# Unscaled expert queries, norm chains in PSUM, compact score copies in four pieces and position additions on GpSimd, in a two-block transformer kernel

## The chip, the cores and the metric

The kernel runs on one core of a Trainium2 chip, as one program. The metric is its device time in microseconds (us), the median of three runs. The engines are TensorE (PE: matmuls, and PEld: its weight loads), VectorE (DVE), ScalarE (ACT), GpSimd (POOL) and SyncE (SP, which issues most DMAs).

## The reference

256 tokens of width 1024 go through two blocks in float32. The first has an HGRN2 linear recurrence beside stick-breaking attention, and a feed-forward layer; the second has gated linear attention (GLA) beside a sparse attention (NSA) with compressed keys, cross attention over a memory of 256 rows, and an expert layer (PEER). What bears on the change:

```python
def rms_norm(x, gain):
    y = x32 * lax.rsqrt(jnp.mean(x32 * x32, axis=-1, keepdims=True) + EPS) * gain
...
    o_hg = rms_norm(o_hg, hg_out_norm[layer]).reshape(b, s, HG_WIDTH)   # 8 heads of 128
    o_hg = o_hg * jax.nn.sigmoid(hg)
    y_hg = o_hg @ w_hg_out[layer]
...
    mixed = jax.nn.sigmoid(ga) * y_hg + jax.nn.sigmoid(gb) * y_sb
    x = x + mixed @ w_o[layer]
...
    o = rms_norm_2(o, out_norm).reshape(B, T, GLA_HEADS * GLA_DV)       # GLA, 4 heads of 128
    return o * jax.nn.silu(gr)
...
def _compress(kv, pos, w1, w2):                                          # 15 blocks of 32 keys
    blocks = kv[:, idx] + pos[None, None, :, None, :]
    return jax.nn.gelu(blocks @ w1) @ w2
...
def peer_ffn(hn, wq, subkeys, down, up):                                 # hn: normed with norm_ffn
    q = (xt @ wq).reshape(N, H, 2, PEER_DKEY // 2)                       # 8 heads
    s = jnp.einsum('nhpd,hpkd->nhpk', q, subkeys)
    s_half, i_half = lax.top_k(s, K)                                     # 16 of 128, then 16 of 16 x 16
    ...
    act = gelu(einsum('cd,chkd->chk', xc, down[ec])) * gate              # all 16384 experts are read
```

## The kernel before, in words

**Weights and main line.** Every linear layer is computed in split precision: a weight is a high part (`whi`) and a low part (`wlo`), and so is the activation, and `mm3` (L395) gives three matmuls for each tile. SP streams the weights by DMA in blocks of 128 x 2048 (`wraw`, `halves`); each half of a block is split into `whi` by ACT (L331) and `wlo = wraw - whi` (L334) by POOL or DVE: every `pool_every`-th half goes to POOL, and none where it is 0. Three `whi` and three `wlo` buffers stand between the splits and PE. `run` takes the halves in the order of a plan; the matmuls of a half are its chunk.

**Background.** After each chunk `step_bg` advances up to `bg_steps` steps of generators in two lanes. They hold the recurrences, attentions, norms of heads and the expert routing, each a few small instructions between two `yield`s. `finish` drains a lane and `drain_bg` both. A scheduler then orders the instructions of each engine; on the chip each engine runs its own list in that order.

**Norms.** `squares` sums the squares of a row on ACT, `row_scales` adds the two halves, and `rstd`/`rsqrt` make the reciprocal root: DVE computes the mean (`v`), ACT takes Ln and Exp (L464, L465: `r`), and DVE makes one Newton step, r * (1.5 - 0.5 r r v) (L467 to L471: `t`, `rs`), on small tiles in SBUF. `diag` (L503) puts a row's scales on a diagonal (`dg`), so that PE scales and transposes in one. `transpose_split` (L481) transposes with the unit matrix in `consts` and splits the result (L453 on ACT, L454 on DVE). `lin_out` normalizes the heads of a linear recurrence: for each of the two 128-token tiles one chain, then the scaling (L754, L757) and the gate (L755). `ev_sbo` (L976, L977) joins the outputs of the two mixers, `ga + ps * gb`.

**Recurrences.** `dyadic` walks the recurrences by halving: `spread` (L668) copies eight pieces of compact scores (`near`) into the score tiles (`S`) on ACT, without a `yield` between them.

**Compress.** `compress` (L1175) adds the position vectors to the keys and values: eight additions of 64 x 240 into `blk` on DVE. POOL is otherwise used for `wlo`, for memsets and at the very end.

**Experts.** `residual` adds the cross attention's output (weights `w_xo`) to `x`, `norm_full` normalizes and transposes it into `px`, and `w_pq` (8 heads, 24 matmuls each) reads it; then come the scores of each head (`psw<-subk,pq`), top 16 on DVE, routing and one-hot tiles in the background, the down stage (128 blocks of 24 matmuls of 256 columns, `psv`) and the up stage (128 of 12 matmuls of 512 columns, `psacc<-whi,Chl`).

Of the kernel before, what the change touches and what calls it, by code (L numbers as in the profile page):

```python
# [206 lines left out]
class Kern:  # L207
# [224 lines left out]
    def feat_mm(self, ps, x, hi, lo):  # L432
        xh, xl = x
        for kt in range(KT):
            s = slice(kt * P, (kt + 1) * P)
            self.mm3(ps, hi[:, s], lo[:, s], F(xh, kt), F(xl, kt), kt == 0, kt == KT - 1)
# [19 lines left out]
    def rstd(self, ss, n, inv):  # L456
        v = self.small(n, "v")
        self.nc.vector.tensor_scalar(v, ss, inv, EPS, ALU.mult, ALU.add)
        return self.rsqrt(v, n)

    def rsqrt(self, v, n):
        nc = self.nc
        r = self.small(n, "r")
# [32 lines left out]
    def row_scales(self, ss):  # L496
        s2 = self.small(2, "nss2")
        self.nc.vector.tensor_add(s2, ss[:, 0:2], ss[:, 2:4])
        return self.rstd(s2, 2, 1.0 / D)
# [6 lines left out]
    def norm_full(self, x, ss, gain, hi, lo):  # L506

        v = self.small(2, "v")
        self.nc.vector.scalar_tensor_tensor(v, ss[:, 2:4], 1.0 / D, ss[:, 0:2], ALU.mult, ALU.add)
        r = self.rsqrt(v, 2)  # L510
# [34 lines left out]
    def residual(self, gain, hold):  # L545

        nc = self.nc

        def ev(g, t, ps):
            s = slice(g * 512, (g + 1) * 512)  # L550
            nc.vector.tensor_add(self.x[t][:, s], ps, self.x[t][:, s])
            if not gain:
                if g == 0 and t == 0:
                    hold["ss"] = self.small(4, "nss")
                ss = hold["ss"]
                if g == 1 and t == 1:
                    sq = self.a2((P, 512), name="sqx")
                    nc.vector.tensor_tensor_reduce(out=sq, in0=self.x[t][:, s], in1=self.x[t][:, s], scale=1.0,
                                                   scalar=0.0, op0=ALU.mult, op1=ALU.add, accum_out=ss[:, 3:4])
                else:  # L560
                    self.squares(self.x, g, ss, (t,))
                if g == 0 and t == 1:
                    nc.vector.tensor_scalar(ss[:, 0:2], ss[:, 0:2], 1.0 / D, EPS, ALU.mult, ALU.add)
            elif t == 1:
                if g == 0:
                    hold.update(self.norm_begin())
                self.norm_part(hold, self.x, g, gain)
                if g == 1:
                    self.norm_end(hold)
        return ev  # L570

    def setup(self):
# [17 lines left out]
        self.none = self.cp.tile([P, P], F32, name="none")  # L590
        nc.gpsimd.memset(self.none, -1.0)
# [27 lines left out]
    def dyadic(self, k, q, p, H, heads, gscale, S, dep):  # L619
# [44 lines left out]
        def spread():  # L664
            for t in range(2):
                for j in range(0, P, SUB):
                    b = slice(j, j + SUB)
                    nc.scalar.activation(S[t][b, :, b].rearrange("p (g n) w -> p g n w", g=ng),  # L668
                                         near[b, :, t * n:(t + 1) * n, :], AF.Copy)

# [16 lines left out]
        for m in LEVELS + (P,):  # L687
# [17 lines left out]
            if m < P:  # L705
# [12 lines left out]
                if m >= SUB:  # L718
                    blocks(z, m)
                else:  # L720
                    scores(z, z, m)
                    if 2 * m == SUB:
                        yield
                        spread()
# [10 lines left out]
    def lin_out(self, S, v, at, dst, order, gated=False):  # L735
        nc = self.nc
        H = 4
        for t in range(2):
# [9 lines left out]
            ss = self.small(4, "oss")  # L748
            nc.scalar.activation(sq, ps, AF.Square)
            nc.vector.tensor_reduce(ss, sq, AX.X, ALU.add)  # L750
            r = self.rstd(ss, 4, 1.0 / P)
            o = dst[t][:, at:at + 512].rearrange("p (h n) -> p h n", h=H)
            if gated:
                nc.vector.tensor_mul(o, o, r.rearrange("p (h o) -> p h o", o=1).to_broadcast([P, H, P]))  # L754
                nc.vector.tensor_mul(o, ps, o)  # L755
            else:
                nc.vector.tensor_mul(o, ps, r.rearrange("p (h o) -> p h o", o=1).to_broadcast([P, H, P]))  # L757
            yield
# [20 lines left out]
    def hgrn_out(self, oh):  # L779
        yield from self.sigmoid3(self.hg)  # L780
        for gi in range(2):
            yield from self.lin_out(self.S[gi], self.hi, gi * 512, self.hg, (0, 1, 2, 3), True)
# [5 lines left out]
    def sb_norm(self, name, gain, scale):  # L788
# [9 lines left out]
        v, r = self.small(32, "v", bufs=2), self.small(32, "r", bufs=2)  # L798
        nc.vector.tensor_scalar(v, st[:, 0, :], 1.0 / 64, EPS, ALU.mult, ALU.add)
        nc.scalar.activation(r, v, AF.Ln)  # L800
        nc.scalar.activation(r, r, AF.Exp, scale=-0.5)
        nc.scalar.activation(st[:, 1, :], r, AF.Square)
        nc.vector.tensor_mul(st[:, 2, :], st[:, 1, :], v)
        nc.vector.tensor_scalar(st[:, 2, :], st[:, 2, :], -0.5, 1.5, ALU.mult, ALU.add)
        nc.vector.tensor_mul(st[:, 3, :], st[:, 2, :], r)
# [78 lines left out]
    def block1(self):  # L884
# [58 lines left out]
        def start_sb():  # L943
            self.finish(1)
            self.pool_every = 2
# [6 lines left out]
            self.osbh, self.osbl = self.feat(name="osbh"), self.feat(name="osbl")  # L952
# [5 lines left out]
        def hg_out():  # L958
            X["hg"] = (self.feat(name="oh"), self.feat(name="ol"))
            return self.hgrn_out(X["hg"])  # L960
# [10 lines left out]
        def ev_sbo(g, t, ps):  # L971
# [4 lines left out]
            nc.vector.tensor_mul(self.gb[t][:, s], ps, self.gb[t][:, s])  # L976
            nc.vector.tensor_add(m, m, self.gb[t][:, s])  # L977
# [153 lines left out]
    def gla_out(self):  # L1131
        nc = self.nc
        yield from self.gla_gate()
        self.o_gla = self.pair(512, "ogla")
        yield from self.lin_out(self.S["gla"], self.gv, 0, self.o_gla, (0, 2, 1, 3))
        for t in range(2):
            nc.vector.tensor_mul(self.o_gla[t], self.o_gla[t], self.gr[t])
            yield
        g = self.col("glan")
        for j in range(0, 4, 2):  # L1140
            ps = self.bank("w", (P, 2, T))
            for q in range(2):
                for t in range(2):
                    nc.tensor.transpose(ps[:, q, t * P:(t + 1) * P], self.o_gla[t][:, (j + q) * P:(j + q + 1) * P],
                                        self.const("ident"))
# [9 lines left out]
    def compress(self):  # L1155
# [6 lines left out]
        for n, src in both:  # L1162
# [6 lines left out]
            for g in range(2):  # L1169
                for par in range(2):  # L1170
# [4 lines left out]
                    nc.vector.tensor_add(blk[b, :, g * 15:(g + 1) * 15], v,  # L1175
# [135 lines left out]
    def block2(self):  # L1311
# [82 lines left out]
        N4, N5 = {}, {}  # L1394
# [15 lines left out]
        self.N5 = N5  # L1410
# [4 lines left out]
        self.lin_tok(lambda: self.xo, d["w_xo"], self.residual(None, N5), kouter=True)  # L1415
# [32 lines left out]
    def peer(self):  # L1448
# [6 lines left out]
        def begin():  # L1455
# [7 lines left out]
            x = [[self.ap.tile([P, 4, T], F32R, name=f"px{i}{j}") for j in range(2)] for i in range(2)]  # L1463
            X["x"] = x
            self.norm_full(self.x, self.N5["ss"], "ffn", *x)
# [5 lines left out]
            self.pool_every, self.bg_steps = 1, PQS  # L1471
        self.call(begin)

# [17 lines left out]
        def score(h, q):  # L1491
# [6 lines left out]
            for p in range(2):  # L1498
                nc.scalar.activation(sc[:, p, :, :], pb[p], AF.Copy)
# [5 lines left out]
        self.lin_feat(lambda: X["x"], d["w_pq"], ev_q)  # L1505
# [103 lines left out]
        def build():  # L1609
            io = self.iota.rearrange("p (o n) -> p o n", o=1).to_broadcast([P, 4, P])  # L1610

            def hot(n):
                (r, gl), m = self.rt[n // 32], n % 32 * 4
                o1 = self.ap.tile([P, 4, P], F32R, tag="oh1", bufs=2, name=self.name("oh"))
                o2 = self.ap.tile([P, 4, 2, P], F32R, tag="oh2", bufs=2, name=self.name("oh"))
# [40 lines left out]
        def routing():  # L1656
            self.rt = []
            self.open_acc(2)
            self.bg_steps = 1
# [104 lines left out]
A4, A2 = 21, 12  # L1764
# [34 lines left out]
```

## Time and profile before

| what | value |
|---|---|
| median of 3 runs | 1608.6 us (1606.46 to 1608.62) |
| profiled execution: its own time, its span | 1608.43 us, 1606.4 us |
| PE busy | 1569.1 us, 98% of the span |
| DVE, ACT, POOL busy | 937.9, 957.6, 755.2 us |
| mean granted clock of PE | 0.993 of full |
| HBM | 191 GB/s over the span |

The span is what the trace covers; the execution's own time has 2.0 us more. Matmuls overlap, so a busy PE in a window says only that it had work. Stretches in which PE did nothing stand in the view of waits, by what ended them. A granted clock of 1.00 in a window is 2.4 GHz; where a window shows less, part of it was at 1.2 GHz.

### The profile page before, as it was taken

The page shows a single profiled execution, that of the slowest core. Times are in us where ns is not written, and L with a number is a line of the kernel's source. Part 1 is how long each engine was busy: PE and PEld are TensorE (multiplying, and loading weights), DVE is VectorE, ACT ScalarE, POOL GpSimd, SP SyncE. Part 2 cuts the span into 40 slices and gives each one's busy share as a digit, 9 for nine tenths or more (in the row PEclk, how much of TensorE's full clock was granted, in tenths as well). Part 3 has the DMA queues.
Part 4 walks back from the last instruction along what each step waited for, and adds up shares of the span by engine and source line. Part 5 has one row for each costly group of instructions (what it writes and reads, how often), then busy time and mean ns, then how long its engine had stood idle before and what let it go on. Part 6 is the DMA issues. An engine that isn't in the chain of part 4 may idle for free. (4 is left out here: it accounts for less than half of the span.)

```text
span 1606.4 us, 28986 instructions
## 1 busy us (share of the span) xinstructions
PE 1569.1 (98%) x11228; PEld 1391.1 (87%) x11228; DVE 937.9 (58%) x2051; ACT 957.6 (60%) x1792; POOL 755.2 (47%) x334
## 2 busy tenths in 40 slices
PE   8999999999999998999999999999999999999997
PEld 8877777879999997779799999999988888898986
DVE  5355446556333466855568559888666665644345
ACT  7688765645444565765454558888755554554454
POOL 3775123433444432323157876767744444444443
PEclk9999999999999998999999999999999999999999
DMA  6543234556555462324335766776776878655552
GB/s 230 181 158 133 80 117 147 190 177 227 204 186 184 163 246 104 132 101 151 137 125 180 221 218 218 234 241 228 249 274 234 334 242 310 233 204 184 184 200 101
DMA packets 52869, 307.70 MB, mean 192 GB/s; under 512 B 5715, under 2 KB 7292, under 8 KB 21500
## 3 DMA queue, kind: packets, MB, share of 16 engines
q1 hardware_dynamic: 51648, 304.06, 55.2%
q8 instruction: 88, 1.44, 0.4%
q10 hardware_dynamic: 1084, 1.80, 0.4%
q14 instruction: 49, 0.40, 0.1%
HBM read 284.59 MB, written 22.56 MB: 191 GB/s over the span
## 5 line engine op out<-in xcount | busy, mean ns | idle before, releaser
L334 POOL TENSOR_TENSOR wlo<-wraw,whi 128x1024 fp32r<-128x1024 f32 (+1 forms) x310 | 746.0, 2408 | 837.6 <-ACT whi L331 821.0
L331 ACT ACTIVATE whi<-wraw 128x1024 fp32r<-128x1024 f32 (+1 forms) x489 | 516.7, 1057 | 466.2 <-PE psacc L395 268.4
L395 PE MATMUL psv<-px,whi 128*128 128x256 f32 x2048 | 367.0, 280 | 1.3 <-ACT A L1676 1.2
L395 PE MATMUL psacc<-whi,Chl 128*128 128x512 f32 x1024 | 324.3, 396 | 0.0
L395 PEld LDWEIGHTS psv<-px,whi 128*128 128x128 f32 x2048 | 315.1, 188 | 3.6 <-ACT A L1676 1.7
L334 DVE TENSOR_TENSOR wlo<-wraw,whi 128x1024 fp32r<-128x1024 f32 (+1 forms) x179 | 223.3, 1248 | 160.2 <-ACT whi L331 160.2
L395 PE MATMUL psv<-px,wlo 128*128 128x256 f32 x1024 | 286.3, 280 | 0.0
L395 PEld LDWEIGHTS psacc<-whi,Chl 128*128 128x128 f32 x1024 | 192.4, 188 | 45.8
L395 PE MATMUL psacc<-wlo,Chl 128*128 128x512 f32 x512 | 202.5, 396 | 0.0
L451 DVE TENSOR_TENSOR Chl<-C,Chl 128x256 fp32r<-128x256 f32 x128 | 103.9, 812 | 159.8 <-PE psacc L395 152.5
L395 PEld LDWEIGHTS psv<-px,wlo 128*128 128x128 f32 x1024 | 192.5, 188 | 0.0
L395 PE MATMUL psacc<-whi,xh 128*128 128x512 f32 (+1 forms) x304 | 121.5, 400 | 0.0
L395 PE MATMUL psacc<-wlo,xh 128*128 128x512 f32 (+1 forms) x304 | 118.5, 390 | 0.4 <-POOL wlo L334 0.4
L395 PE MATMUL psacc<-whi,xl 128*128 128x512 f32 (+1 forms) x304 | 118.6, 390 | 0.0
L395 PEld LDWEIGHTS psacc<-wlo,Chl 128*128 128x128 f32 x512 | 96.2, 188 | 22.5
L395 PE MATMUL psacc<-xh,wlo 128*128 128x256 f32 x352 | 102.2, 291 | 4.2 <-DVE wlo L334 4.2
L395 PE MATMUL psacc<-xh,whi 128*128 128x256 f32 x352 | 103.9, 295 | 0.6 <-ACT whi L331 0.6
L395 PE MATMUL psacc<-xl,whi 128*128 128x256 f32 x352 | 101.8, 289 | 0.0
L395 PE MATMUL psw<-xh,whi 128*128 128x256 f32 x352 | 99.8, 283 | 0.0
L395 PE MATMUL psw<-xh,wlo 128*128 128x256 f32 x352 | 99.6, 283 | 0.0
L395 PE MATMUL psw<-xl,whi 128*128 128x256 f32 x352 | 99.6, 283 | 0.0
L395 PEld LDWEIGHTS psacc<-xh,wlo 128*128 128x128 f32 x352 | 69.1, 197 | 4.5 <-DVE wlo L334 4.4
(415 smaller groups left out, 2644.7 us busy)
## 6 DMA issues: line engine op xcount, KB each, us to landing
wraw<-in_w_dn_dram SPq DMA_DIRECT2D x64, 1024.0 KB, 5.5
wraw<-in_w_up_dram SPq DMA_DIRECT2D x64, 1024.0 KB, 4.9
wraw<-in_w_f_dram SPq DMA_DIRECT2D x33, 1024.0 KB, 4.8
Ad<-A SPq DMA_DIRECT2D x22, 512.0 KB, 6.5
A<-Ad SPq DMA_DIRECT2D x22, 512.0 KB, 3.4
Gd<-stg SPq DMA_DIRECT2D x16, 512.0 KB, 6.3
G<-Gd SPq DMA_DIRECT2D x16, 512.0 KB, 6.6
wraw<-in_w_hq_dram SPq DMA_DIRECT2D x4, 1024.0 KB, 4.8
```

The source lines that it names most:

```text
L331: nc.scalar.activation(hi[:, :n], r, AF.Copy)
L334: eng.tensor_sub(lo[:, :n], r, hi[:, :n])
L395: return self.nc.tensor.matmul(out, l, r, start=start, stop=stop)
L451: nc.vector.tensor_sub(lo, src, hi)
```

## The change

- The chains of the norms (`newton`) keep the operands of their DVE steps in a PSUM bank `st`, one operand of each product being in PSUM; the square of r is done on ACT. `diag` goes from DVE to ACT. `lin_out` makes one chain for both token tiles (eight columns), and multiplies with scales that lie in PSUM; GLA's gate is applied in it.
- `spread` yields after every two copies.
- The position additions of `compress` go from DVE to POOL.
- `ev_sbo` multiplies into the PSUM operand.
- `pool_every` is 0 from the start of the stick-breaking attention until `hg_out`, which sets 2 again; before it was 2 throughout. So 8 low splits go from POOL to DVE there.
- The experts start without the norm: `ev_last` transposes `x` times the gain, unscaled by rows, in two halves (`keep`, `xg`); `w_pq` runs on that; the copies of the scores from PSUM are scaled by the row (16 copies of 128 x 256 become 32 of 128 x 128). The scaled `px`, which the down stage reads, is made in the background (`norm_scaled`). Heads 0 and 1 begin with the first half of `x`. `bg_steps` is 2 during the scores.

The diff, cut to its core:

```diff
+    def newton(self, st, inv, out):
+        nc, n = self.nc, st.shape[2]
...
+        nc.vector.tensor_scalar(v, st[:, 0, :], inv, EPS, ALU.mult, ALU.add)
         nc.scalar.activation(r, v, AF.Ln)
         nc.scalar.activation(r, r, AF.Exp, scale=-0.5)
-        t = self.small(n, "t")
-        nc.vector.tensor_mul(t, r, r)
-        nc.vector.tensor_mul(t, t, v)
-        nc.vector.tensor_scalar(t, t, -0.5, 1.5, ALU.mult, ALU.add)
-        o = self.small(n, "rs")
-        nc.vector.tensor_mul(o, r, t)
-        return o
+        nc.scalar.activation(st[:, 1, :], r, AF.Square)
+        nc.vector.tensor_mul(st[:, 2, :], st[:, 1, :], v)
+        nc.vector.tensor_scalar(st[:, 2, :], st[:, 2, :], -0.5, 1.5, ALU.mult, ALU.add)
+        nc.vector.tensor_mul(out, st[:, 2, :], r)
...
-        self.nc.vector.tensor_scalar(dg, self.const("ident"), r[:, t:t + 1], None, ALU.mult)
+        self.nc.scalar.activation(dg, self.const("ident"), AF.Copy, scale=r[:, t:t + 1])
...
                                          near[b, :, t * n:(t + 1) * n, :], AF.Copy)
+                    if j % (2 * SUB):
+                        yield
...
-            self.pool_every = 2
+            self.pool_every = 0
...
-            nc.vector.tensor_mul(self.gb[t][:, s], ps, self.gb[t][:, s])
-            nc.vector.tensor_add(m, m, self.gb[t][:, s])
+            nc.vector.tensor_mul(ps, ps, self.gb[t][:, s])
+            nc.vector.tensor_add(m, m, ps)
...
-                    nc.vector.tensor_add(blk[b, :, g * 15:(g + 1) * 15], v,
+                    nc.gpsimd.tensor_add(blk[b, :, g * 15:(g + 1) * 15], v,
...
+        def ev_last(g, t, ps):
+            s = slice(g * 512, (g + 1) * 512)
+            nc.vector.tensor_add(self.x[t][:, s], ps, self.x[t][:, s])
+            if g == 0 and t == 1:
+                self.transpose_split(self.x, *([w] for w in self.keep), self.col("ffn"), range(4))
+                self.ss = self.small(4, "nss")
+                self.squares(self.x, 0, self.ss)
...
+        def rows_done():
+            self.transpose_split(self.x, *X["g"], self.col("ffn"), range(4, KT))
+            self.squares(self.x, 1, self.ss)
+            X["r"] = self.row_scales(self.ss)
+            self.go(self.norm_scaled(self.x, X["r"], "ffn", *X["x"]), 1)
...
-                nc.scalar.activation(sc[:, p, :, :], pb[p], AF.Copy)
+                for t in range(2):
+                    nc.scalar.activation(sc[:, p, t, :], pb[p][:, t, :], AF.Copy, scale=X["r"][:, t:t + 1])
```

On ACT, around the compact copies of GLA, the list before has both tiles' copies (`S`, eight in two rows) in one piece, ahead of the two weight splits `whi`:

```order
L697 ACTIVATE psw_6569<-gp_6078 128x256
L450 ACTIVATE nqr_6497<-psacc_6471 128x256
L715 ACTIVATE psw_6572<-gp_6078 128x8
L668 ACTIVATE S_6087<-near_6094 32x4x32 x4
L668 ACTIVATE S_6088<-near_6094 32x4x32 x4
L715 ACTIVATE psw_6572<-gp_6078 128x8
L331 ACTIVATE whi_6607<-wraw_6605 128x1024
L331 ACTIVATE whi_6685<-wraw_6605 128x1024
```

and now (the same names with other numbers):

```order
L331 ACTIVATE whi_6498<-wraw_6437 128x1024
L683 ACTIVATE psw_6390<-hqs_6062 128x256
L683 ACTIVATE psw_6393<-gp_6050 128x256
L701 ACTIVATE psw_6396<-gp_6050 128x16 x2
L450 ACTIVATE nqr_6469<-psacc_6443 128x256
L652 ACTIVATE S_6059<-near_6066 32x4x32 x4
L652 ACTIVATE S_6060<-near_6066 32x4x32 x2
L331 ACTIVATE whi_6537<-wraw_6535 128x1024
L450 ACTIVATE nqr_6469<-psacc_6502 128x256
L652 ACTIVATE S_6060<-near_6066 32x4x32 x2
L331 ACTIVATE whi_6610<-wraw_6535 128x1024
```

One weight split now stands ahead of the last two copies, and the chunk's `nqr` copies between them.

On DVE, at the same place, the list before has the position additions (`blk`) ahead of a low split:

```order
L662 COPY_PREDICATED near_6094<-masks,psw_6430 128x4x16
L1175 TENSOR_TENSOR blk_6509<-kvc_6065,miscs 64x16x15
L451 TENSOR_TENSOR nqr_6498<-psacc_6471,nqr_6497 128x256
L1175 TENSOR_TENSOR blk_6509<-csw_6506,miscs 64x16x15 x2
L1175 TENSOR_TENSOR blk_6509<-kvc_6065,miscs 64x16x15
L1175 TENSOR_TENSOR blk_6526<-kvc_6066,miscs 64x16x15
L1175 TENSOR_TENSOR blk_6526<-csw_6523,miscs 64x16x15 x2
L1175 TENSOR_TENSOR blk_6526<-kvc_6066,miscs 64x16x15
L334 TENSOR_TENSOR wlo_6533<-wraw_6465,whi_6532 128x1024
```

and now DVE's low split follows the predicated copies directly, and POOL has the additions among its own splits:

```order
L334 TENSOR_TENSOR wlo_6230<-wraw_6227,whi_6229 128x1024
L1147 MEMSET blk_6481 128x16x2
L1155 TENSOR_TENSOR blk_6481<-kvc_6037,miscs 64x16x15
L1155 TENSOR_TENSOR blk_6481<-csw_6478,miscs 64x16x15 x2
L1155 TENSOR_TENSOR blk_6481<-kvc_6037,miscs 64x16x15
L1147 MEMSET blk_6492 128x16x2
L1155 TENSOR_TENSOR blk_6492<-kvc_6038,miscs 64x16x15
L1155 TENSOR_TENSOR blk_6492<-csw_6489,miscs 64x16x15
L334 TENSOR_TENSOR wlo_6440<-wraw_6437,whi_6439 128x1024
L1155 TENSOR_TENSOR blk_6492<-csw_6489,miscs 64x16x15
L1155 TENSOR_TENSOR blk_6492<-kvc_6038,miscs 64x16x15
```

Two of the eight additions stand behind a split that waits for its `whi`.

On DVE, at the start of the experts, the list before has the last additions to `x` (L551), the last sum of squares, one low split and then the norm's chain (`v`, `t`, `rs`, `dg`):

```order
L334 TENSOR_TENSOR wlo_8476<-wraw_8457,whi_8475 128x1024
L551 TENSOR_TENSOR x_83<-psacc_8387,x_83 128x512
L551 TENSOR_TENSOR x_84<-psacc_8388,x_84 128x512
L558 ISA sqx_8494,nss_8446<-x_84 128x512
L334 TENSOR_TENSOR wlo_8499<-wraw_8496,whi_8498 128x1024
L509 SCALAR_TENSOR_TENSOR v_8518<-nss_8446 128x2
L467 TENSOR_TENSOR t_8523<-r_8520 128x2
```

and now low parts of `keep` (first half) and a low split ahead of those additions, and a low split and four low parts of `xg` behind them, ahead of the chain (`psw_8530`, `n`, `rs`):

```order
L454 SCALAR_TENSOR_TENSOR keep_89<-psw_8419,cols,keep_88 128x256
L334 TENSOR_TENSOR wlo_8450<-wraw_8431,whi_8449 128x1024
L1393 TENSOR_TENSOR x_83<-psacc_8344,x_83 128x512
L1393 TENSOR_TENSOR x_84<-psacc_8345,x_84 128x512
L334 TENSOR_TENSOR wlo_8470<-wraw_8467,whi_8469 128x1024
L454 SCALAR_TENSOR_TENSOR xg_8490<-psw_8510,cols,xg_8489 128x256
L454 SCALAR_TENSOR_TENSOR xg_8490<-psw_8519,cols,xg_8489 128x256
L454 SCALAR_TENSOR_TENSOR xg_8490<-psw_8510,cols,xg_8489 128x256
L454 SCALAR_TENSOR_TENSOR xg_8490<-psw_8519,cols,xg_8489 128x256
L493 TENSOR_TENSOR psw_8530<-psw_8530,nss_8428 128x2
L460 TENSOR_SCALAR n_8534<-psw_8530 128x2
```

PE has there, in place of its wait for `dg`, the transposes of `x`'s second half and then head matmuls that read `keep` and `xg`.

## Rows read from the trace of the kernel before

**Rows 1.** the page: span, and busy time of the engines

```profile
span 1606.4 us, 28986 instructions
...
PE 1569.1 (98%) x11228; PEld 1391.1 (87%) x11228; DVE 937.9 (58%) x2051; ACT 957.6 (60%) x1792; POOL 755.2 (47%) x334
```

**Rows 2.** view of waits, all of PE: what PE waited for: us, times, longest

```profile
PE psw L395 <- DVE dg L503: 4.5, 1, 4.5
PE psacc L395 <- DVE wlo L334: 4.2, 1, 4.2
PE psw L481 <- DVE ol L454: 2.5, 1, 2.5
PE psw L1279 <- DVE ogla L757: 2.3, 1, 2.3
PE psw L481 <- DVE ga L977: 2.3, 2, 1.3
PE psw L851 <- DVE sbr L451: 2.0, 2, 1.3
...
PE psw L481 <- DVE t L467: 1.0, 1, 1.0
```

**Rows 3.** windows: busy us (instructions) of each engine, PEclk, DMA share, GB/s

```profile
160.00:200.00 40.00, 38.72 (x241) 29.85 (x240) 17.32 (x26) 30.75 (x63) 7.09 (x3) 1.00 0.23 80
253.00:260.00 7.00, 4.50 (x17) 3.51 (x17) 6.25 (x13) 3.62 (x7) 0.74 (x1) 0.76 0.47 151
618.00:628.00 10.00, 9.42 (x114) 7.54 (x115) 5.81 (x14) 4.63 (x19) 0.00 (x0) 0.52 0.61 211
804.00:812.00 8.00, 7.55 (x51) 7.56 (x52) 3.70 (x9) 3.31 (x7) 0.00 (x0) 0.79 0.14 54
```

**Rows 4.** timeline of POOL at three places: start, us, instruction, idle before

```profile
192.57 2.37 POOL L334 TENSOR_TENSOR wlo<-wraw,whi 128x1024 fp32r<-128x1024 f32 x1 [12.92 <-ACT whi L331]
...
614.46 2.46 POOL L334 TENSOR_TENSOR wlo<-wraw,whi 128x1024 fp32r<-128x1024 f32 x1 [8.45 <-ACT whi L331]
...
676.55 2.36 POOL L334 TENSOR_TENSOR wlo<-wraw,whi 128x1024 fp32r<-128x1024 f32 x1 [5.11 <-ACT whi L331]
```

**Rows 5.** timeline of DVE at the same three places

```profile
193.16 2.21 DVE L451 TENSOR_TENSOR sbr<-sbe,sbr 128x384 fp32r<-128x384 f32 x1 [0.92 <-PE psw L851]
...
613.61 1.15 DVE L1175 TENSOR_TENSOR blk<-csw,miscs 64x240 f32<-64x240 f32 x2
614.77 2.50 DVE L1175 TENSOR_TENSOR blk<-kvc,miscs 64x240 f32<-64x240 f32 x1
617.30 1.23 DVE L334 TENSOR_TENSOR wlo<-wraw,whi 128x1024 fp32r<-128x1024 f32 x1
...
676.60 2.33 DVE L467 TENSOR_TENSOR t<-r 128x4 f32<-128x4 f32 x1 [0.59 <-ACT r L465]
```

**Rows 6.** groups by form, DVE, 318 to 340: busy us, mean ns, idle before

```profile
L977 DVE TENSOR_TENSOR ga<-ga,gb 128x512 f32<-128x512 f32 x4 | 5.0, 1254 | 0.1
L976 DVE TENSOR_TENSOR gb<-psacc,gb 128x512 f32<-128x512 f32 x4 | 2.7, 685 | 2.1 <-PE psacc L395 2.1
```

**Rows 7.** timelines of POOL and DVE: a norm chain with operands in PSUM

```profile
98.35 4.77 POOL L334 TENSOR_TENSOR wlo<-wraw,whi 128x1024 fp32r<-128x1024 f32 x2
...
100.63 0.20 DVE L803 TENSOR_TENSOR psw<-psw,v 128x32 f32<-128x32 f32 x1 [3.13 <-ACT psw L802]
```

**Rows 8.** timeline of ACT at the compact copies

```profile
610.48 2.55 ACT L668 ACTIVATE S<-near 32x128 f32<-32x128 f32 x8
...
613.27 2.00 ACT L331 ACTIVATE whi<-wraw 128x1024 fp32r<-128x1024 f32 x2
```

**Rows 9.** groups by form, POOL, 1560 to the end

```profile
L1725 POOL TENSOR_TENSOR o<-x,gfin 128x512 f32<-128x512 f32 x2 | 2.6, 1286 | 5.7 <-DVE x L1720 4.2 <-DVE v L1729 1.5
```

**Rows 10.** timeline of PE, experts' start; L481 by source (min/median/max ns, first, last)

```profile
804.45 3.17 PE L395 MATMUL psw<-dg,x 128*128 128x128 f32 x16 [4.51 <-DVE dg L503]
...
L481 PE MATMUL psw<-consts,wraw x16: 270/272/273, 308.5 to 310.1; 128*128 128x128 f32 x16
```

More of the change, by code (lines that the diff above doesn't have):

```diff
@@ L430, in lin_tok, with feat_mm @@
                     chunk(g, h)
-    def feat_mm(self, ps, x, hi, lo):
+    def feat_mm(self, ps, x, hi, lo, ks=range(KT)):
         xh, xl = x
-        for kt in range(KT):
+        for kt in ks:
             s = slice(kt * P, (kt + 1) * P)
@@ L454, in split @@
             nc.vector.scalar_tensor_tensor(lo, src, scale, hi, ALU.mult, ALU.subtract)
[L456 to L463, printed above, removed]
+    def newton(self, st, inv, out):
+        nc, n = self.nc, st.shape[2]
+        v, r = (self.sp.tile([P, n], F32, tag=f"n{n}", bufs=2 if n > 8 else 4, name=self.name("n")) for _ in range(2))
+        nc.vector.tensor_scalar(v, st[:, 0, :], inv, EPS, ALU.mult, ALU.add)
         nc.scalar.activation(r, v, AF.Ln)
         nc.scalar.activation(r, r, AF.Exp, scale=-0.5)
[L466 to L472 removed]
+        nc.scalar.activation(st[:, 1, :], r, AF.Square)
+        nc.vector.tensor_mul(st[:, 2, :], st[:, 1, :], v)
+        nc.vector.tensor_scalar(st[:, 2, :], st[:, 2, :], -0.5, 1.5, ALU.mult, ALU.add)
+        nc.vector.tensor_mul(out, st[:, 2, :], r)
     def transpose_split(self, src, hi, lo, gain=None, ks=range(KT)):
@@ L551, in ev @@
             nc.vector.tensor_add(self.x[t][:, s], ps, self.x[t][:, s])
[L552 to L564, printed above, removed]
+            if t == 1:
                 if g == 0:
@@ L590, in setup @@
         self.none = self.cp.tile([P, P], F32, name="none")
+        self.keep = [self.cp.tile([P, 4, T], F32R, name=f"keep{i}") for i in range(2)]
         nc.gpsimd.memset(self.none, -1.0)
@@ L723, in dyadic @@
                         yield
-                        spread()
+                        yield from spread()
             else:
@@ L747, in lin_out @@
             sq = self.a2((P, H, P), name="osq")
-            ss = self.small(4, "oss")
             nc.scalar.activation(sq, ps, AF.Square)
-            nc.vector.tensor_reduce(ss, sq, AX.X, ALU.add)
-            r = self.rstd(ss, 4, 1.0 / P)
-            o = dst[t][:, at:at + 512].rearrange("p (h n) -> p h n", h=H)
[L753 to L758, printed above, removed]
+            nc.vector.tensor_reduce(st[:, 0, t * H:(t + 1) * H], sq, AX.X, ALU.add)
+            out.append(ps)
+            yield
+        self.newton(st, 1.0 / P, st[:, 3, :])
+        yield
+        for t, ps in enumerate(out):
+            o = dst[t][:, at:at + 512].rearrange("p (h n) -> p h n", h=H)
+            r = st[:, 3, t * H:(t + 1) * H].rearrange("p (h o) -> p h o", o=1).to_broadcast([P, H, P])
+            nc.vector.tensor_mul(o, o, r)
+            nc.vector.tensor_mul(o, ps, o)
+        yield
     def hgrn(self, gi):
@@ L797, in sb_norm @@
             yield
[L798 to L805, printed above, removed]
+        self.newton(st, 1.0 / 64, st[:, 3, :])
         for t in range(2):
@@ L951, in start_sb @@
             nc.scalar.activation(self.negm, self.const("sbneg"), AF.Copy)
-            self.osbh, self.osbl = self.feat(name="osbh"), self.feat(name="osbl")
+            self.osbh, self.osbl = ([t, self.a4((P, 4, T), F32R, name="osb")] for t in self.keep)
             return self.stick()
@@ L958, in hg_out @@
         def hg_out():
+            self.pool_every = 2
             X["hg"] = (self.feat(name="oh"), self.feat(name="ol"))
@@ L1133, in gla_out @@
         yield from self.gla_gate()
[L1134 to L1138, printed above, removed]
+        yield from self.lin_out(self.S["gla"], self.gv, 0, self.gr, (0, 2, 1, 3))
         g = self.col("glan")
@@ L1462, in begin @@
             self.open_acc()
-            x = [[self.ap.tile([P, 4, T], F32R, name=f"px{i}{j}") for j in range(2)] for i in range(2)]
-            X["x"] = x
-            self.norm_full(self.x, self.N5["ss"], "ffn", *x)
+            X["x"] = [[self.ap.tile([P, 4, T], F32R, name=f"px{i}{j}") for j in range(2)] for i in range(2)]
+            X["g"] = [[w, self.pa((P, 4, T), "xg", dt=F32R)] for w in self.keep]
             self.subk = self.pa((P, 8, P), "subk")
@@ L1504, in score, with pq, fn @@
                 yield
-        self.lin_feat(lambda: X["x"], d["w_pq"], ev_q)
+        first = []
+        def pq(c):
+            def fn(hi, lo, i):
+                h = 2 * c + i
+                first.append((h, self.acc((P, T)), hi, lo))
+                self.feat_mm(first[-1][1], X["g"], hi, lo, range(4))
+                if h == 0:
+                    rows_done()
+                    return
+                for h, ps, hi, lo in first:
+                    self.feat_mm(ps, X["g"], hi, lo, range(4, KT))
+                    ev_q(h, ps)
+                first.clear()
+            return fn
+        for c in range(4):
+            self.w(d["w_pq"][c], pq(c))
         def small(shape, name, dt=F32, bufs=1):
@@ L1760, in peer @@
                 nd += 1
-A4, A2 = 21, 12
+A4, A2 = 20, 12
 NA, RUNAHEAD, KEEP = 5, 50, 3
```

35 lines of the change are left out of this document (19 added, 16 removed).

## The prediction

> **What bounds the kernel now.** I read the page first: PE is busy for 1569.1 of 1606.4 us [rows 1], so 37.3 us is all the time in which it has nothing, and whatever the change does on other engines counts only where PE then waits less, or more. The view of waits comes next. The seven rows in [rows 2] name DVE as the releaser and add up to 18.8 us, half of that idle time. (The rest, at the program's head and tail and in crumbs, stands where the change moves nothing on PE's path.) Third come the windows behind the longer of these waits: the granted clock is 0.76 from 253 to 260 us, 0.52 from 618 to 628 and 0.79 from 804 to 812 [rows 3], so part of these windows runs at 1.2 instead of 2.4 GHz. What that costs is the window times the missing share: 7 x 0.24 = 1.7 us, 10 x 0.48 = 4.8 us and 8 x 0.21 = 1.7 us. The wait for `ogla` (2.3 us) and those of ev_sbo and the stick-breaking attention (1.3 at most) have no such stretch behind them. Together 18.8 + 8.2 = 27 us are within reach of the change, 1.7% of the time.
>
> **Why DVE is late.** The timelines show one pattern. A DVE operation whose two operands both lie in SBUF, and which starts while POOL subtracts a low split, ends when POOL ends. At 676.60 the product r * r on 128x4 takes 2.33 us, and POOL's split runs from 676.55 to 678.91; at 193.16 an `sbr` takes 2.21 us beside a split that ends at 194.94; at 614.77 one position addition takes 2.50 us beside a split that ends at 616.92, where two others took 1.15 [rows 4, 5]. An operation with one operand in PSUM does not do so: in the head norms' chain the product `psw * v` takes 0.20 us in the middle of a POOL split [rows 7], and in ev_sbo the product with `psacc` means 0.685 us on the same shape on which the addition of two SBUF tiles means 1.254 [rows 6]. The Trainium skill, in "SBUF — State Buffer", section "Who interferes with whom", says the same: a VectorE instruction with two SBUF inputs contends with a GpSimd instruction that reads SBUF, one with at most one does not. The trace agrees (2.33 against 0.20 us), and by that rule the additions that move to POOL can hold DVE up in their turn; that is a rival below.
>
> **The change part by part.**
>
> *Stick-breaking.* With pool_every at 0 no POOL split runs beside `sbr`. PE's two waits for it go: -2.0 us [rows 2]. The price is eight more low splits on DVE, 8 x 1.23 = 9.8 us [rows 5]. From 160 to 200 DVE is busy for 17.3 of 40 us [rows 3], so the room is there; its cover is PE's queue of three split buffers. I take nothing for it, and keep the other end as a rival.
>
> *HGRN output.* The chain's products get an operand in PSUM (0.20 instead of up to 2.33 us), and one chain replaces two of each group. Order on DVE leaves the chain ready ahead of the transposes. Both waits go (`t` 1.0, `ol` 2.5 [rows 2]) and with them the slow clock (1.7): -5.2 us.
>
> *ev_sbo.* Four additions shrink from 1.254 to 0.685 us on average: 2.3 us, all of it on the pair of waits of 2.3 us: -2.2 us, a tenth left for the wake-up.
>
> *Compress and the score copies.* PE's wait of 4.2 us is for a DVE split, the one that ends at 618.53 [rows 5], so it began near 614.4. Two things made that split late. On ACT the eight score copies held 2.55 us, and the two weight splits behind them end only at 615.27 [rows 8]; on DVE the additions ended at 617.27, and the low split took 1.23 more [rows 5]. Had only the additions gone, DVE could begin at 615.3 and end at 616.5, and the wait would still be some 2.1 us; had only the copies been cut, it would be as before. The change does both: a weight split now stands between the copies, and DVE's low split follows the predicated copies. The wait goes, and the slow clock with it: -4.2 - 4.8 = -9.0. Against it stand new waits of PE for recurrence operands that the cut copies push back; nothing at least, and at most the two copies that now stand behind a split (about 1.0 + 0.3 us each, from rows 8), of which I take 0.7. Term: -8.3 us.
>
> POOL's additions have no row. Below stand 0.57 us, what DVE takes (1.15 for two, [rows 5]); above stands 1.29 us, POOL's own two-operand product on 128x512 [rows 9]. From POOL's 2.37 us on 1024 columns [rows 4] and 1.29 on 512 the time goes as 0.2 us + 2.1 ns a column, which at 240 gives 0.70 us: an estimate, and the value that I take. Six of them, 4.2 us, lie in the 8.45 us that POOL idled ahead of its split at 614.46 [rows 4]; two stand behind that split and end near 618.3, about when PE, without its wait, asks for `blk`. The Trainium skill, in "GPSIMD Engine Reference", section "Engine selection", calls a two-input element-wise operation on GpSimd about twice as slow as on VectorE. By that rule eight additions take 9.2 instead of 5.6 us, the last two end 0.9 us later, and the sum would be at most that much worse; no run before shows such an addition there.
>
> *GLA output.* The chain that was held for 2.33 us at 676.60 is free, and the gate is in the scaling: the wait of 2.3 goes, -2.3 us.
>
> *Start of the experts.* Away go the wait for `dg` (4.5) and its slow clock (1.7): -6.2. Added on PE are 16 transposes; sixteen such begin between 308.5 and 310.1 [rows 10], 0.107 us each, so +1.7 (the 32 products with `dg` still run, later). New waits: (a) the second half's transposes need the last additions to `x`, one of 128x512 like ev_sbo's, 0.69, behind a low split; PE has head matmuls of the first half to do, and 0.5 is left; (b) matmuls on `xg` need its low parts, which stand behind another low split of 1.23 and behind each other, 1.7; (c) the scaled `px` needs `dg`, now on ACT behind a weight split of 1.0 and score copies, 1.2. That is 3.4, each piece an estimate from the orders; nothing at least, 4.5 + 1.7 at most (the wait as it was). Term: -6.2 + 1.7 + 3.4 = -1.1 us. Nothing else of the expert stages changes on PE: the smaller score copies (ACT) and the faster background are off its path.
>
> **Sum.** -2.0 - 5.2 - 2.2 - 8.3 - 2.3 - 1.1 = -21.1. The profiled execution took 1608.43 us (span 1606.4 and 2.0 around it), the median is 1608.6; so 1587.4, and I forecast **1587 us**.
>
> **Rivals.**
>
> *POOL keeps the hold on compress (A).* If POOL's additions cost 1.29 us and more, or hold DVE's low split as POOL's splits hold DVE now, PE waits there again, now for `blk` or the split. For it: two additions behind a split, and two SBUF operands on both engines. Against it: the idle 8.45 us, and six additions that, begun at 606.0 where POOL's idle begins, are over by 611 even at 0.8 us. The compress term falls from -8.3 to about 0: 1595.7.
>
> *The experts' start gets its own long wait (B).* Three waits fall close together, each on DVE or ACT queues with a weight split in them; if two join, the wait is as long as the one of 4.5 that had a slow clock behind it. For it: four low parts, a split and the chain in a row on DVE. Against it: PE has 24 matmuls of the first half between. The term goes from -1.1 to 1.7 + 4.5 + 1.7 - 6.2 + about 1 = +2.7: 1591.2.
>
> *PSUM operands don't free the chains (C),* and the change does there not what it says: the long operations come from queueing, and HGRN output, GLA output and ev_sbo keep their waits (9.7): 1597. Against it speak [rows 6, 7].
>
> *DVE becomes the bound in the stick-breaking stretch (D), slower than before.* All 16 low splits of `hi` and `hg` now go to DVE, which runs its list in order; where its head waits for ACT's `sbe` or PE's `psw`, the low split behind it waits too, and PE after it. It decides from 21.1 / 16 = 1.3 us a split on; at 1.6 us each it costs 25.6: 1613. DVE's share of 17.3 in 40 speaks against it, and so does the single wait of 0.92 [rows 5] in front of an `sbr`.
>
> **Chances.** Forecast 0.58 (its own range 1583 to 1590), B 0.17, A 0.11, C 0.07, D 0.03; in 0.04 two of A to C come together, near 1601. So 8 times in 10 the time lies between **1581 and 1597**: below, where new waits of 3.4 and 0.7 come to nothing and the small crumbs shrink, above by A and C. A measurement of this kernel can tell about 0.2% (3.2 us) from no change. Faster by more than that: 0.93; within: 0.03; slower: 0.04.
>
> **What the changed profile would show.** PE's waits for `sbr`, `t`, `ol`, `ga`, `ogla` and for a DVE split gone or below 0.5 us each; PEclk 1.00 in the windows at 250 and 610; position additions on POOL near 0.70 us; the chains' DVE products at 0.2 us; at the experts' start several waits of 0.5 to 1.9 us with no slow clock; span near 1585. I am wrong if a wait above 3 us appears at a new place, if PE waits for DVE splits between 155 and 235, or if `blk` releases PE.

## The result, and the profile after

The changed kernel takes 1597.4 us (median of four runs, 1594.87 to 1597.56) where the kernel before takes 1607.5 beside it: a ratio of 0.9934 (interval 0.9922 to 0.9947), 10.1 us less. The forecast was 1587: the sign and nearly every wait came out as described, but only half of the 21.1 us arrived, and the time lies 0.4 us past the upper edge of the range of 1581 to 1597.

The page of the changed kernel (span, busy time), answering to [rows 1]:

```profile
span 1595.7 us, 29039 instructions
...
PE 1575.2 (99%) x11244; PEld 1390.5 (87%) x11244; DVE 917.5 (57%) x2021; ACT 972.0 (61%) x1839; POOL 741.3 (46%) x334
```

PE's idle time went from 37.3 to 20.5 us, by 16.8, while the span fell by 10.7. So PE is busy 6.1 us longer than before, although only 16 small transposes were added and the slow clock went. That is the difference which the forecast does not have.

The view of waits, all of PE, answering to [rows 2]:

```profile
PE psw L475 <- DMA consts<-in_consts_dram: 4.6, 1, 4.6
PE psw L475 <- DMA x<-in_x_dram: 1.3, 1, 1.3
PE psw L1259 <- ACT pcT L1255: 1.1, 1, 1.1
PE psv L395 <- ACT A L1686: 1.1, 1, 1.1
PE psacc L395 <- POOL wlo L334: 1.0, 1, 1.0
PE psw L395 <- DVE mx L1237: 1.0, 1, 1.0
PE psacc L395 <- ACT whi L331: 0.6, 1, 0.6
PE psw L395 <- DVE hz L684: 0.5, 1, 0.5
PE psw L475 <- DVE x L1393: 0.3, 1, 0.3
```

All seven waits of [rows 2] are gone. New are `pcT` and `mx` (sparse attention, 1.1 and 1.0), a wait of 1.0 for a POOL split in one piece (before, three of 0.4 at most), and at the experts' start a wait of 0.3 for `x`, in place of the 3.4 of the working.

Windows at the four places (busy us and instructions of each engine, PEclk, DMA share, GB/s), answering to [rows 3]:

```profile
160.00:200.00 40.00, 39.92 (x244) 30.46 (x242) 20.35 (x32) 31.23 (x62) 0.00 (x0) 1.00 0.26 88
245.00:260.00 15.00, 15.00 (x83) 12.75 (x82) 12.36 (x24) 8.30 (x17) 4.82 (x2) 1.00 0.46 157
600.00:630.00 30.00, 30.00 (x391) 24.75 (x390) 16.57 (x48) 21.42 (x62) 11.10 (x7) 1.00 0.43 143
785.00:812.00 27.00, 26.56 (x199) 23.97 (x197) 17.60 (x73) 17.99 (x43) 9.46 (x4) 1.00 0.41 144
```

The clock is full in all of them, and DVE has room in the stick-breaking stretch (20.35 of 40). Two operations by source line (min/median/max ns, first and last start), the chain's product and ev_sbo's addition, and POOL's additions as groups by form (busy us, mean ns, idle):

```profile
L464 DVE TENSOR_TENSOR psw<-psw,n x11: 161/169/200, 18.2 to 796.4; 128x2 f32<-128x2 f32 x6, 128x8 f32<-128x8 f32 x3, 128x32 f32<-128x32 f32 x2
...
L961 DVE TENSOR_TENSOR ga<-ga,psacc x4: 687/687/689, 317.3 to 330.8; 128x512 f32<-128x512 f32 x4
...
L1155 POOL TENSOR_TENSOR blk<-csw,miscs 64x240 f32<-64x240 f32 x4 | 3.8, 943 | 0.2
L1155 POOL TENSOR_TENSOR blk<-kvc,miscs 64x240 f32<-64x240 f32 x4 | 2.9, 728 | 0.2
```

With an operand in PSUM no product of the chains takes over 0.20 us (before, up to 2.33), and the additions of ev_sbo take 0.69 (before, 1.254 on average). POOL's addition takes 0.73 us where 0.70 was estimated, 1.3 times the 0.57 of DVE; one of 1.61 us lifts the other group's mean.

Where the busy time grew, the starts of matmuls show. The period of a matmul is taken here as the time from its start to the start of the next, averaged over a stretch. The timeline of PE in the feed-forward layer (96 matmuls of 256 columns, then 24 of 512, then the next 256), and in the late down stage (48 of 256), changed kernel:

```profile
396.75 0.28 PE L395 MATMUL psw<-xh,whi 128*128 128x256 f32 x1
...
408.14 0.39 PE L395 MATMUL psacc<-whi,fh 128*128 128x512 f32 x1
...
413.71 0.28 PE L395 MATMUL psw<-xh,whi 128*128 128x256 f32 x1
...
1418.73 0.40 PE L395 MATMUL psv<-px,whi 128*128 128x256 f32 x2
...
1424.42 0.40 PE L395 MATMUL psacc<-whi,Chl 128*128 128x512 f32 x1
```

From start to start: 11.39 / 96 = 118.6 ns, 5.57 / 24 = 232 ns, 5.69 / 48 = 118.6 ns. The same stretches in the trace of before:

```profile
402.69 0.28 PE L395 MATMUL psw<-xh,whi 128*128 128x256 f32 x1
...
414.20 0.40 PE L395 MATMUL psacc<-whi,fh 128*128 128x512 f32 x1
...
419.67 0.28 PE L395 MATMUL psw<-xh,whi 128*128 128x256 f32 x1
...
1419.03 0.40 PE L395 MATMUL psv<-px,whi 128*128 128x256 f32 x2
...
1424.63 0.39 PE L395 MATMUL psacc<-whi,Chl 128*128 128x512 f32 x1
```

They give 119.9, 227.9 and 116.7 ns. No engine is waited for in them and the clock is full; the matmul itself has another period.

### The profile page after: what moved, and what is told of

Read it like the earlier page. It is cut to its first block, busy times and chain, and to the rows that moved or that the text cites. A ratio compares the mean times of both kernels' runs of the same rounds, so it can differ in the third digit from the quotient of the medians.

```text
span 1595.7 us, 29039 instructions
## 1 busy us (share of the span) xinstructions
PE 1575.2 (99%) x11244; PEld 1390.5 (87%) x11244; DVE 917.5 (57%) x2021; ACT 972.0 (61%) x1839; POOL 741.3 (46%) x334
## 4 chain that ended last, share of the span: by engine, by line
PE 93%; ACT 2%; issue 2%; DVE 2%; POOL 1%; DMA 0%; SPq 0%; ACTq 0%; POOLq 0%
PE psacc L395 54%; PE psv L395 23%; PE psw L395 14%; POOL wlo L334 1%; PE psw L475 1%; ACT whi L331 1%; PE psw L834 0%; DMA x<-in_x_dram 0%; ACT pr L1240 0%; DVE wlo L334 0%; DVE sm L1242 0%; PE psw L835 0%; PE psw L798 0%; DVE pr L1244 0%; DVE pr L1237 0%
## 5 line engine op out<-in xcount | busy, mean ns | idle before, releaser
L334 POOL TENSOR_TENSOR wlo<-wraw,whi 128x1024 fp32r<-128x1024 f32 x302 | 725.3, 2403 | 840.7 <-ACT whi L331 779.3
L334 DVE TENSOR_TENSOR wlo<-wraw,whi 128x1024 fp32r<-128x1024 f32 x187 | 234.9, 1257 | 169.3 <-ACT whi L331 169.2
L395 PE MATMUL psacc<-wlo,xh 128*128 128x512 f32 (+1 forms) x304 | 119.9, 395 | 1.0 <-POOL wlo L334 1.0
L395 PEld LDWEIGHTS psacc<-xh,whi 128*128 128x128 f32 x352 | 67.7, 192 | 1.5 <-ACT whi L331 0.9
```

The source lines that it names most:

```text
L334: eng.tensor_sub(lo[:, :n], r, hi[:, :n])
L395: return self.nc.tensor.matmul(out, l, r, start=start, stop=stop)
```

## The experiments

**Placement put back, and taken away.** The new small tiles of `newton` sit between the weight splits (`whi`, `wlo`) and the activations in SBUF. Counted in the addresses of the built program, activations of the blocks lay 0 bytes modulo 512 from the weight splits before and 384 after; `px` and `Chl` lay 288 before and 160 after. (`keep` adds 8192 bytes in front of the splits, a multiple of 512.) One edit moves everything behind the scratch tile:

```diff
-        self.junk = self.xp.tile([P, 512], BF16, name="junk")
+        self.junk = self.xp.tile([P, 576], BF16, name="junk")[:, 0:512]
```

on the changed kernel (the padded run), and with 704 in place of 576 on the kernel before (the mirror run).

> The changed kernel, with 128 bytes per partition more in a scratch tile, so that x and everything allocated behind it (activations, px, Chl) lies 128 bytes further from the weight splits, at the same distance modulo 512 bytes as before the change; nothing else differs. Theory P (placement): the period of a matmul depends on how its two operands lie to each other in SBUF, and the change moved them. Then the 512-column matmuls of the blocks go from 232 back to 227 ns (some 1600 of them, -8 us), those of the down stage from 118.6 to 116.8 ns (3072, -4 to -5.5 us), the 256-column ones of the feed-forward layer from 118.6 to 120.0 (some 1400, +2 us): about -10, 1587 us. Theory A (activity): the longer periods come from what the other engines and the DMAs do at the same time, or from the instruction stream; then nothing changes, 1597 +- 1.

> The kernel before, with 384 bytes per partition more in the same scratch tile, which gives the distances modulo 512 bytes of the changed kernel; nothing else differs. Theory P: the mirror of the run above, 512-column matmuls at 232 ns, down stage at 118.6, feed-forward at 118.6: +10, 1617 to 1618 us. Theory A: 1607.5 +- 1.

The first took 1590.2 us (ratio to before 0.9886, 0.9870 to 0.9903), 7.2 less than the changed kernel by medians and 7.9 by spans; the second 1614.4 (1.0040, 1.0024 to 1.0055), 6.0 more than before. The periods followed. The same places in the padded run (timeline of PE):

```profile
393.38 0.28 PE L395 MATMUL psw<-xh,whi 128*128 128x256 f32 x1
...
404.90 0.40 PE L395 MATMUL psacc<-whi,fh 128*128 128x512 f32 x1
...
410.37 0.28 PE L395 MATMUL psw<-xh,whi 128*128 128x256 f32 x1
...
1411.88 0.40 PE L395 MATMUL psv<-px,whi 128*128 128x256 f32 x2
...
1417.48 0.39 PE L395 MATMUL psacc<-whi,Chl 128*128 128x512 f32 x1
```

11.52 / 96 = 120.0 ns, 5.47 / 24 = 228 ns, 5.60 / 48 = 116.7 ns: all three as in the kernel before. In the mirror run:

```profile
403.91 0.28 PE L395 MATMUL psw<-xh,whi 128*128 128x256 f32 x1
...
415.30 0.39 PE L395 MATMUL psacc<-whi,fh 128*128 128x512 f32 x1
...
420.87 0.28 PE L395 MATMUL psw<-xh,whi 128*128 128x256 f32 x1
...
1424.17 0.40 PE L395 MATMUL psv<-px,whi 128*128 128x256 f32 x2
...
1429.80 0.40 PE L395 MATMUL psacc<-whi,Chl 128*128 128x512 f32 x1
```

They are 118.6, 232 and 117.3 ns. Same instructions, same order, another address: theory A falls. The weight splits lie ahead of the padding, at one place modulo 512 in all runs here, so these runs do not tell whether the distance of the two operands counts, or the place of the activations alone.

The sizes were set too large (10 expected, 7 and 6 measured). Matmuls of the same weights, set against each other in the traces of the changed kernel and of the padded run, lie 3.7 us apart at the start of the down stage, where 6 net were set, and 4.2 more at the end (4 to 5.5 set). Why the blocks give less than the periods promise no run shows.

**Two parts alone.** The compress part and the stick-breaking part, put into the kernel before, with no tile moved:

```diff
-                    nc.vector.tensor_add(blk[b, :, g * 15:(g + 1) * 15], v,
+                    nc.gpsimd.tensor_add(blk[b, :, g * 15:(g + 1) * 15], v,
...
+                    if j % (2 * SUB):
+                        yield
```

```diff
-            self.pool_every = 2
+            self.pool_every = 0
...
         def hg_out():
+            self.pool_every = 2
```

> The kernel before with the position additions on GpSimd and the score copies cut into four pieces, and nothing else of the change; tiles lie where they lay. Prediction's term: PE's wait of 4.2 us for a DVE split and the slow clock behind it go, -9.0, with new waits of up to 0.7: 1599 us. Rival (GpSimd keeps the hold): PE waits there for blk or a split, 1607 us.

> The kernel before with no low split on GpSimd during the stick-breaking attention (pool_every 0 from its start until the HGRN output), and nothing else of the change. Prediction's term: the two waits for sbr go, -2.0: 1605.5 us. Rival D (DVE becomes the bound there): PE waits for DVE splits between 155 and 235 us, each 1 us or more, 1615 us or more.

The pair at compress gave 1607.0 (0.9991, 0.9981 to 1.0001): 1.4 us, not 8.3. The stick-breaking part gave 1608.0 (0.9997, 0.9984 to 1.0011), which tells neither -2.0 nor nothing apart. In its trace the waits for `sbr` are gone, but the two of the HGRN output (1.0 and 2.5, [rows 2]) are now one of 2.4, so its profile says little beyond itself; rival D's waits for DVE splits between 155 and 235 us did not appear. Its view of waits:

```profile
PE psacc L395 <- DVE wlo L334: 4.2, 1, 4.2
PE psw L481 <- DVE hg L755: 2.4, 1, 2.4
```

**The pair taken apart**, one run each:

> The kernel before with the position additions on GpSimd, copies uncut. By the prediction's working ScalarE's copies then set the weight split: PE's wait for a DVE split falls from 4.2 to some 2.1 us, and the slow clock behind it goes or shrinks: 5 to 7 us less than before. If the additions have no part in it, the wait stays 4.2.

> The kernel before with the score copies cut, additions on DVE. By the prediction's working the additions still hold DVE's split, and the wait stays near 4 us: span within 1 us of before. If the cut copies cost as the pair's run suggests (waits for sbr 3.9 instead of 2.0, for pcT 2.3 and hz 1.8 instead of 0.6), the same new waits of PE appear here, and not with the additions alone.

The additions alone: 1601.0 us, 6.9 less, with no wait for a DVE split left. The cut copies alone: 1611.2, 3.3 more (a single run, while the kernel before ranges over 7.6 us, so the waits tell more than the time), with these rows in the view of waits:

```profile
PE psw L853 <- DVE sbr L451: 3.8, 4, 1.5
PE psw L395 <- issue: 2.7, 2, 2.4
...
PE psw L1281 <- ACT pcT L1277: 2.3, 2, 1.2
...
PE psw L395 <- DVE hz L700: 1.8, 3, 1.1
```

Against 2.0 for `sbr`, 0.6 for `hz` and none for `pcT` in the kernel before. Each extra `yield` is a background step, four in each recurrence, so the recurrences end later and what follows them in the lanes meets other neighbours. My working had it the wrong way round three times. The copies did not hold DVE's split once the additions were away (in that run ScalarE makes the split at 605.61, ahead of the copies at 609.46). Cutting them was not free. And with only the copies cut the wait for a DVE split did not stay near 4 us: it is gone, and the row with `issue` has 2.4 us in its place. They lie ahead of the matmuls that read `blk`, which start at 621.04, right behind the last position addition on DVE (to 620.94).

**The norm chains and ev_sbo alone, and the up stage's operand moved.** The first puts `newton`, `lin_out`, `diag` and ev_sbo of the diff into the kernel before, with 576 in the scratch tile, so that distances modulo 512 stay. The second is the padded changed kernel with

```diff
             self.idx = [self.ap.tile([P, 8, 2, 16], U32, name=f"idx{t}") for t in range(2)]
+            gap = self.ap.tile([P, 56], F32, name="gap")
+            nc.gpsimd.memset(gap, 0.0)
```

> The kernel before with the norm chains in PSUM (row scales, head norms, lin_out with one chain for both tiles, GLA's gate in it, diag on ScalarE except at the experts' start) and ev_sbo's product in PSUM, and nothing else of the change; 128 bytes are added to the scratch tile, so that with the new small tiles everything behind lies 512 bytes further and keeps its distance to the weight splits modulo 512. Prediction's terms: HGRN output -5.2, ev_sbo -2.2, GLA output -2.3: -9.7, 1598 to 1599 us. Rival C (the chains were late by queueing): 1607 to 1608, with the waits for t, ol, ga and ogla as before.

> The changed kernel with the 128 bytes of the first run (activations of the blocks at distance 0 modulo 512 from the weight splits), and in the expert stages a gap of 224 bytes ahead of the up stage's activations, so that Chl, too, lies at distance 0; px stays at 288. Theory P: the up stage's 1536 matmuls of 512 columns go from 233.3 to 226.7 ns, -10: 1580 us. If distance 0 matters only for the tiles of the blocks, or the weights' DMAs set the up stage's pace, 1590.

The chains: 1596.7 (0.9930, 0.9914 to 0.9947), 11.2 us less where 9.7 was expected, with the waits for `t`, `ol`, `ga` and `ogla` gone; rival C falls. The aligned up stage: 1579.6 (0.9823, 0.9807 to 0.9840), 10.6 below the run with 128 bytes alone. Windows of 100 us in the up stage, the changed kernel and then this one:

```profile
1200.00:1300.00 100.00, 100.00 (x430) 80.44 (x429) 60.88 (x91) 51.20 (x72) 43.19 (x18) 1.00 0.78 279
```

```profile
1200.00:1300.00 100.00, 100.00 (x443) 82.81 (x442) 64.73 (x93) 52.78 (x74) 43.90 (x19) 1.00 0.79 283
```

430 matmuls before the gap, 443 with it: 233 against 226 ns (start to start in the traces, 233.3 and 226.7), and the DMAs keep up.

The chains' run also shows something about the slow clock. Its wait at compress is the one of before, 4.2 us, but the window behind it reads (and below it that of the stick-breaking run, after the same wait):

```profile
612.00:622.00 10.00, 10.00 (x143) 8.00 (x143) 5.99 (x17) 7.22 (x30) 1.77 (x1) 0.85 0.63 211
```

```profile
616.00:626.00 10.00, 8.91 (x137) 7.33 (x137) 6.76 (x15) 5.84 (x22) 0.15 (x1) 0.83 0.65 211
```

0.85 and 0.83 where [rows 3] have 0.52: 10 x 0.15 = 1.5 us given away, not 4.8. Over 50 us around this wait the granted clock is 0.90 in the traces of before and of the two kernels before with padding (5.0 us each), and 0.97 in these two (1.5 us): the slow stretch behind one and the same wait differs. So does the time of the kernel before itself, 1603.2 to 1610.8 over 21 runs of one batch, with mean granted clocks of 0.996 and 0.991 in these two runs: 0.005 x 1607 = 8 us, all of the difference. What decides it no run shows.

**The copies in one piece again, the start alone, and another distance for px.**

> The kernel of the run with Chl aligned (1579.6), with the score copies in one piece again. If the cut copies cost what their run alone showed (3 us), in waits for pcT and mx that the run with Chl aligned still has (1.1 and 1.0), the time falls by 2 to 3: 1577. If the prediction's working holds (ScalarE's copies hold the weight split when they are in one piece), PE waits some 2 us for a DVE split at compress, and the time rises to 1581 or more.

The diff is that of the copies, undone. 1579.5 (0.9829, 0.9811 to 0.9848): no difference that times can tell. The waits for `pcT` and `mx` (2.1) went, and no wait for a DVE split came. Matmuls of the same weights, set against each other in the two traces, lie 1.7 us apart already at 25 us, in the program's head, where the kernels do not differ; behind that the uncut version loses 1.0 in the first block and gains 2.9 in the second. So in the whole change the cut copies are worth nothing, or cost a microsecond or two.

> The kernel before with all of the change but the experts' new start (that stage as before, bg_steps too), padded so that tiles keep their distances modulo 512 of before; to be compared with the changed kernel at the same distances (1590.2). Prediction's term for the start, -1.1: this run at 1591.3. Rival B (the start's new waits and slow clock outweigh, +2.7): 1587.5. The wait of 4.5 for dg and the slow clock behind it should stand here.

1592.0 (0.9906, 0.9887 to 0.9924) against 1590.2 (0.9886): the start gives 1.8 us, near the 1.1 of the working, with the wait of 4.5 for `dg` standing in this run; the two intervals overlap, so times alone make rival B unlikely; the waits exclude it, since 0.4 us for `x` is all that the start has in the padded run.

> The kernel of the run with uncut copies, with px at distance 256 modulo 512 bytes from the weight splits in place of 288 (Chl stays at 0). Matmuls of 256 columns took 120.0 ns at distance 0, 118.6 at 384, 116.8 at 288 and 117.3 to 118.6 at 160, which would fit a least value near 256: 113.3 to 116.8 ns here, 0 to 10 us less than the run with uncut copies. If the distance modulo 512 is not what sets the down stage's period, it comes out of this range, or without a change of the period.

The edit is a `lead` tile of 480 bytes in front of `px` and a gap of 256. 1587.0 (0.9872, 0.9853 to 0.9892), 7.5 more than its base: a miss, outside the range that I gave. Timeline of PE, 48 matmuls:

```profile
1409.78 0.40 PE L395 MATMUL psv<-px,whi 128*128 128x256 f32 x2
...
1415.53 0.40 PE L395 MATMUL psacc<-whi,Chl 128*128 128x512 f32 x1
```

5.75 / 48 = 119.8 ns, the same as at distance 0. That suggests 256 as the modulus, which the last run tests:

> The kernel before with 256 bytes per partition more in the scratch tile: activations of the blocks at distance 256 from the weight splits, px and Chl at 32. Theory P as worded so far (modulo 512): 512-column matmuls of the blocks leave 226.7 ns, and px at 32 is a new point. Theory P modulo 256, which the run with px at 256 suggests (119.9 ns there as at 0): every period stays as before, 226.7 (512 columns, blocks), 120.0 (256 columns, feed-forward), 116.8 (down stage), 233.3 (up stage), and the time 1607 to 1608.

1608.0 us in a single run (before beside it 1606.8). Timeline of PE:

```profile
402.21 0.28 PE L395 MATMUL psw<-xh,whi 128*128 128x256 f32 x1
...
413.72 0.40 PE L395 MATMUL psacc<-whi,fh 128*128 128x512 f32 x1
...
419.19 0.28 PE L395 MATMUL psw<-xh,whi 128*128 128x256 f32 x1
...
1418.72 0.40 PE L395 MATMUL psv<-px,whi 128*128 128x256 f32 x2
...
1424.32 0.39 PE L395 MATMUL psacc<-whi,Chl 128*128 128x512 f32 x1
```

11.51 / 96 = 119.9 ns, 5.47 / 24 = 227.9 ns, 5.60 / 48 = 116.7 ns, and 233.3 ns in the up stage, each as before: modulo 256.

## Why the prediction was right in its waits and wrong by half in its size

- **What bounds, and why DVE is late: right.** Every wait named went in the full change, and those of the chains in the run of the chains alone. Two readings were loose: the `sbr` and the addition of [rows 5] end 0.4 us after POOL's split and not with it, and the product of [rows 7] runs across the seam of two POOL splits. The 0.20 us itself holds: in the changed kernel no product of the chains takes longer.
- **"Nothing else of the expert stages changes on PE", and the sum's silence on the blocks: the step that failed.** The sum left out that the new tiles move the operands. That term is +7 to +8 us by the padded run, the larger part of the 11 us missing. The order of instructions, on which I worked, cannot show it. That 1597.4 still lies at the edge of the range is luck: the range was opened upward for A and C, and neither happened.
- **Terms at unmoved distances.** In the padded run the time is 18.2 us below before, where 21.1 were set. Matmuls of the same weights, set against each other in the traces of before and of that run, show by stage: 9.3 us gained up to the feed-forward layer (2.0 + 5.2 + 2.2 = 9.4 were set), 7.0 from there to the cross attention's queries (8.3 + 2.3 = 10.6 set), 1.0 lost near the end of `w_xo` (nothing set there), 3.0 gained behind it (1.1 set). The 1.0 belongs to the start of the experts: eight of its 16 transposes, those of the first half of `x`, stand there:

```profile
778.47 0.44 PE L475 MATMUL psw<-consts,x 128*128 128x128 f32 x2
...
779.22 0.82 PE L475 MATMUL psw<-consts,x 128*128 128x128 f32 x6
```

- **Chains, ev_sbo and stick-breaking: right.** The chains' part alone, with GLA's 2.3, gives 11.2 where 9.7 was set. Set against before in the same way, its trace has 7.6 us up to the feed-forward layer (7.4 set) and 2.3 at the GLA output (2.3 set). Another 2.6 lie at compress, where the chains change nothing and the clock is the less slow one shown above, so this part of the 11.2 is luck. The 2.0 of the stick-breaking part is within the 9.4; by times alone it is not told from nothing.
- **Compress, -8.3: mis-sized by the cut copies**, the term that is short in the second block. They were taken as a gain with new waits of 0.7. They add waits of 2.1 (`pcT`, `mx`), and without the rest of the change they take most of the gain back. The 7.0 of the stage above become 9.9 of the 10.6 in the trace with the copies in one piece. The additions alone give 8.5 at the place itself, near the whole of wait and slow clock, and 6.9 in the end: 1.6 go again behind the wait for `ogla`, where the clock is 0.83 over 10 us in that run and 1.00 in before.
- **Start of the experts, -1.1: mis-sized the other way**, 1.8 by times and 3.0 - 1.0 = 2.0 by the traces. The new waits are 0.3 to 0.4 and not 3.4; with that the working would have given -6.2 + 1.7 + 0.4 = -4.1, and the 2 us between are not accounted for.
- **Rivals:** A to D fell as they were put: A by the run of the additions alone, B by the waits at the start, C by the chains alone, D by the waits of the stick-breaking run. The case that happened, a matmul that takes longer, was none of them.

## What to carry to other kernels

Before costing a change, compare the addresses of matmul operands as well as the order of instructions: a few small new tiles cost 7 to 8 us here, more than any one of the waits that went, and 224 bytes of padding gave 10.6 us. When PE's busy time rises without new matmuls at full clock, count matmuls in a pure stretch: the period tells. Take the price of a slow-clock stretch from several executions, and test edits that are made together also alone.

## What the runs showed of the hardware that was not expected

The period of a matmul depends on where its activations lie in SBUF, modulo 256 bytes. The table has the distance of its two operands, activations minus weight split, both of type fp32r (the type that the splits are written in). Since the weight splits lay at one place modulo 256 throughout, the place of the activations alone would sort the runs in the same way. That 256 is the modulus rests on two pairs of places (0 and 256, 32 and 288).

| distance modulo 256 | 512 weight columns moving | 256 activation columns moving |
|---|---|---|
| 0 | 226.7 ns (227.9 over a run of 24, its first step included) | 119.9 ns |
| 32 | 233.3 ns | 116.7 ns |
| 128 | 232 ns | 118.6 ns |
| 160 | 233.3 ns | 117.3 to 118.7 ns |

So the best place for one kind is the worst for the other. At 160 both values occur within one trace: in the changed kernel the chunks of 24 have 117.4 ns at 944 us, 118.7 at 972 and 118.6 in the late down stage, where the mirror run has 117.3. So the place is not the whole of it; why it matters no run here shows. The best kernel of the study has the blocks' activations and `Chl` at 0 and `px` at 32 (288): 1579.6 us, a ratio of 0.9823 to before against 0.9934 for the change.
